# Four token groups per z tile, a 64-column product ahead of a run of 256, and backward order in every second tile

## The chip, the cores and the metric

The kernel runs on one core of a Trainium2 chip. A core has TensorE (matrix products into PSUM), VectorE, ScalarE and GpSimd, each with its own instruction stream, and SyncE, which like ScalarE issues DMA transfers. The metric is the device time of one execution in microseconds (us). The kernel before took 1241.5 us in the median of three runs, 1241.24 to 1242.45. Outputs are compared with a JAX reference.

## The reference, cut to what matters

One layer with two parallel token mixers, then a feed-forward part. 1024 tokens and 16 meta tokens make T = 1040 rows of width 1024.

```python
h = layer_norm(concat(meta, x))
z = h @ w_in + b_in                       # 1040 x 1024 by 1024 x 3840
q, k, v, c_in, gates = split(z)           # 512 | 128 | 128 | 1024 | 2048 columns
y_attn = swa_sink_attention(q, k, v, ...) @ w_attn_proj
c = c_val * sigmoid(c_gate)               # c_val, c_gate = split(c_in)
y_conv = silu(layer_norm(causal_dwconv(c, 31 taps))) @ w_conv_proj
mixed = sigmoid(g_attn) * y_attn + sigmoid(g_conv) * y_conv
h = layer_norm(alpha * h + mixed @ w_out)
f = (gelu(gate) * up) @ ffn_w_down        # up, gate from causal_dwconv(h @ ffn_w_up, 3 taps)
out = layer_norm(alpha * h + f)[16:]
```

The change lies in `z = h @ w_in` and in the two projections to `y_attn` and `y_conv`.

## The kernel before, in words

**Products.** Every fp32 operand is split into a high part and a low part in the type fp32r, and a product is three matmuls: high by high, high by low, low by high. `product` (L294) does this for a list of terms into one PSUM tile, and a matmul brings its own weight load of 128 x 128. In the trace the three are L298, L302 and L303.

**z.** The 3840 columns of z are 30 tiles of 128. A tile holds its weights still and moves the tokens, so its result has 128 partitions and a column for each token. The normalised input lies transposed in SBUF in 8 chunks of 128 features, high and low parts, chunks 0 to 3 in `RHO` and 4 to 7 in `RHC`; `h0` (L255) gives the slice of a chunk for a range of tokens. The tokens are cut into three groups, `HG` = 0 to 272, 272 to 656, 656 to 1040 (L54). Three tiles (k, v, the first q) are computed at the start in a hand-written order. The other 27 go through `z_tile` (L313), which takes the groups in order, and `z_group` (L306), which runs 8 chunks by 3 matmuls into one of three PSUM buffers (tag "mm") and then calls an eviction. The 27 are eight tiles of the convolution's input (`conv_chunk`, L640: a gate through tanh on ScalarE, then a product with it on VectorE into `cin`), three tiles of q (`q_evac`, L347) and sixteen gate tiles (`gate_tile`, L665: tanh on ScalarE into a staging slot, then a store to `sgd` from ScalarE's DMA queue). Gate and q tiles use `TG` (L321), where the first group starts at token 14 and has 258 columns. `stage` (L325) hands out five staging slots of 400 columns in turn.

**Order.** Instructions stand in each engine's stream as a scheduler puts them, by the priority in `tc.cur_priority` or `rank` and its own times. Attention runs over 8 blocks of 128 queries and two head groups, and its matmuls (`ps_s` scores, `ps_t` transposes, `ps_o` values) are interleaved with those of z tiles, which have the lower rank. `ahead` (L744) names a matmul of the first gate tile behind which the first score matmuls are put. Behind the attention come the rest of the gate tiles, and with them the layer norm of the convolution (`ps_m`).

**Projections.** For each of eight columns m of 128 output features, `branch` (L1122) runs 4 terms (12 matmuls) for the attention branch and 12 for the convolution branch, for each of the four groups of `PG` (258, 256, 256, 256 columns); `merge` (L1130) applies the gates. The tile is `ps_p`. The last column runs all its attention groups first.

**Behind it**, untouched: the product with w_out (`ps_w`), the up-projection by a fast scheme of seven products per tile (`px`, `pz`, `pw`, `py`, L1552, runs of 258 and 256 columns), and the down-projection (L1696, 512 columns).

Of the kernel before, what the change touches and what calls it, by code (L numbers as in the profile page):

```python
# [31 lines left out]
KC = D // P  # L32
# [3 lines left out]
U0 = 14  # L36
# [17 lines left out]
HG = [(0, 272), (272, 656), (656, 1040)]  # L54
UG = [(0, 258), (258, 642), (642, 1026)]

PG = [(0, 258), (258, 514), (514, 770), (770, 1026)]


HW = 514  # L60
# [40 lines left out]
def tile_hybrid_layer(  # L101
# [3 lines left out]
    nc = tc.nc  # L105
# [36 lines left out]
    FA = arena.tile([P, 6144], F, name="FA")  # L142
    RHC = arena.tile([P, 8320], R, name="RHC")
    RHO = arena.tile([P, 8320], R, name="RHO")
# [22 lines left out]
    start = ExitStack()  # L167
# [85 lines left out]


    def h0(k, hl, a, b):  # L255
        g = next(g for g, x in enumerate(HG) if a < x[1])
        x, y = HG[g]
        i, n = (k % 4) * 2 + hl, y - x
        o = i * n + ((6144 if i else 0), 272, 3344)[g]
        return (RHO if k < 4 else RHC)[:, o + a - x:o + b - x]  # L260


    tc.cur_priority = RK_QKV
# [27 lines left out]

    chunks_done = []

    def product(ps, terms, behind=None):  # L294

        n = len(terms)
        for i, (ah, al, bh, bl) in enumerate(terms):
            ins = nc.tensor.matmul(ps, ah, bh, start=i == 0, stop=False)  # L298
            chunks_done.append(ins)
            if i == 0 and behind is not None:  # L300
                after(ins, behind)
            nc.tensor.matmul(ps, ah, bl, start=False, stop=False)  # L302
            last = nc.tensor.matmul(ps, al, bh, start=False, stop=i == n - 1)  # L303
        return last

    def z_group(wt, g, a, b, evac):  # L306
        hi, lo = wt
        ps = pat.tile([P, 512], F, name="ps_z", tag="mm", bufs=3)
        product(ps[:, :b - a], [(hi[:, k], lo[:, k], h0(k, 0, a, b), h0(k, 1, a, b)) for k in range(KC)])
        with rank(RK_EVAC):  # L310
            evac(g, a, b, ps[:, :b - a])

    def z_tile(fill, groups, evac, wt=None):  # L313
        wt = wt or weights([P, KC, P], fill)
        for g, (a, b) in enumerate(groups):
            z_group(wt, g, a, b, evac)

    def in_cols(m):
        return lambda raw: load(raw, w_z[m])

    TG = [(a + U0 if i == 0 else a, b) for i, (a, b) in enumerate(HG)]  # L321

    st_next = [0]

    def stage(n, lo=4104, cnt=5):  # L325
        i = st_next[0] % cnt
        st_next[0] += 1
        return FA[:, lo + i * 400:lo + i * 400 + n]

    tc.cur_priority = RK_QKV + 1000  # L330

# [272 lines left out]
    for a, b in ((0, 400), (400, J_LEN)):  # L604
        ps = pat.tile([P, 512], F, name="ps_v", tag="o" if a == 0 else "t", bufs=1 if a == 0 else 2)
# [5 lines left out]
    wt_c1 = [weights([P, KC, P], in_cols(m)) for m in (11, 7)]  # L611
# [28 lines left out]
    def conv_chunk(c):  # L640
        sig = {}

        def g_evac(g, a, b, ps):
            sig[g] = stage(b - a)

            nc.scalar.activation(sig[g], ps, AF.Tanh, bias=bcol(10 + c), scale=0.5)
            nc.scalar.activation(sig[g], sig[g], AF.Identity, bias=half_, scale=0.5)

        z_tile(in_cols(10 + c), HG, g_evac, wt_c1[0] if c == 1 else None)
        cin = cp.tile([P, 16 + T], F, name="cin", tag="cin")  # L650
        nc.vector.memset(cin[:, 0:16], 0.0)

        def v_evac2(g, a, b, ps):
            nc.vector.scalar_tensor_tensor(cin[:, 16 + a:16 + b], ps, bcol(6 + c), sig[g], OP.add, OP.mult)

        z_tile(in_cols(6 + c), HG, v_evac2, wt_c1[1] if c == 1 else None)
        with rank(RK_CONV + c * 100):
            for j in range(TAPS):
                wc = cdw[:, j * CH + c:j * CH + c + 1]
                if j == 0:  # L660
                    nc.vector.tensor_scalar(acc[c], cin[:, j:j + U], wc, cdwb(c), OP.mult, OP.add)
                else:
                    nc.vector.scalar_tensor_tensor(acc[c], cin[:, j:j + U], wc, acc[c], OP.mult, OP.add)  # L663
# [38 lines left out]
    ps = pat.tile([P, 512], F, name="ps_vm", tag="t", bufs=2)  # L702
# [4 lines left out]
    for q4 in range(2):  # L707
        ps = pat.tile([P, 512], F, name="ps_v4", tag="t", bufs=2)
        for i in range(4):
            c = NMETA + (q4 * 4 + i) * P  # L710
# [30 lines left out]
    tc.cur_priority = RK_Z - 500  # L741
    first_chunk = len(chunks_done)
    gate_tile(0)
    ahead = chunks_done[first_chunk + 2 * KC + 5]  # L744

    tc.cur_priority = RK_ATT

# [255 lines left out]
    def oo(r, hl, a, b):  # L1003
        return OA[:, place(r * 2 + hl, a, b)]
# [114 lines left out]
    for m in range(KC):  # L1119
        hi, lo = weights([P, KC, P], lambda raw: load(raw, w_ab[m]))  # L1120

        def branch(i, g, tag, bufs):  # L1122
            a, b = PG[g]
            ps = pat.tile([P, 512], F, name="ps_p", tag=tag, bufs=bufs)
            rhs = (oo, conv)[i]
            product(ps[:, :b - a], [(hi[:, 4 * i + k], lo[:, 4 * i + k], rhs(k, 0, a, b), rhs(k, 1, a, b))
                                    for k in range(4)])
            return ps[:, :b - a]

        def merge(g, psa, psb):  # L1130
            a, b = PG[g]
            n = b - a
            with rank(RK_EVAC):
                t = gslot()[:, :, :n]
                ins = load(t, dram(sgd, m * P * U + a, [[U, P], [KC * P * U, 2], [1, n]]))

                ta, tb = t[:, 0], t[:, 1]
                nc.vector.scalar_tensor_tensor(ta, ta, 1.0, psa, OP.add, OP.mult)
                nc.vector.scalar_tensor_tensor(tb, tb, 1.0, psb, OP.add, OP.mult)
                nc.vector.tensor_tensor(ta, ta, tb, OP.add)  # L1140
                if g == 0:
                    nc.scalar.mul(pair[:, m, 0:2], ta[:, 0:2], 0.5)
                v = ta[:, n - 256:].rearrange("p (t x) -> p t x", t=2)
                h = mixed2(g, m, 0)
                last_act = nc.scalar.mul(h, v, 0.5)
                nc.vector.scalar_tensor_tensor(mixed2(g, m, 1), v, 0.5, f32(h), OP.mult, OP.subtract)
            return ins, last_act

        if m < KC - 1:
            for g in range(4):  # L1150
                last_gate, last_act = merge(g, branch(0, g, "mm", 3), branch(1, g, "t", 2))
        else:
            pa = [branch(0, g, "mm", 3) if g < 3 else branch(0, g, "s", 2) for g in range(4)]
            for g in range(4):
                last_gate, last_act = merge(g, pa[g], branch(1, g, "t", 2))
        if m in (2, 3):
            raw = (FA[:, 4112:5136], OB[:, 3072:4096])[m - 2]
            load(raw, w_out_v[m + 2])
            prep_wo(m + 2, raw, last_act)
        if m < 4:  # L1160
            early.append(FA[:, W_AT[m]:W_AT[m] + 1024])
            wo_raw[m] = early[m]
            after(load(early[m], w_out_v[m]), last_gate)
        if m > 1:
            with rank(RK_PROJ + 3000):
                two_rows(m - 2)
# [261 lines left out]
    ahead = []  # L1428
# [422 lines left out]
```

## Time and profile before

| | |
|---|---|
| median of 3 runs | 1241.5 us |
| the profiled execution | 1241.26 us |
| its span (first to last instruction) | 1239.5 us |
| TensorE busy | 1229.4 us, 8540 matmuls |
| VectorE busy | 1084.0 us |
| ScalarE busy | 580.0 us |
| z tiles through `z_tile` | about 56 to 408 us of the span |
| of these, interleaved with attention | about 162 to 327 us |
| projections | about 408 to 503 us |

A row of the timeline gives start (us), duration (us), engine, line, operation, output<-inputs, weights, moved operand (partitions x columns), and how many equal instructions in a row it merges. A matmul's duration reaches over the start of the next ones, since they are pipelined; the spacing of starts is what it costs in a stream. "PEld" rows are the weight loads. In the view of waits, a row is engine, tile and line, what it waited for, the total in us, how often, and the longest. In the view by groups, "x48 | 26.1, 543 | 47.7" reads: 48 instructions, 26.1 us busy, 543 ns in the mean, 47.7 us of idle time before them. The mark "(x...)" in the list of engines counts instructions.

### The profile page before, as it was taken

The page shows a single profiled execution, that of the slowest core. Times are in us where ns is not written, and L with a number is a line of the kernel's source. Part 1 is how long each engine was busy: PE and PEld are TensorE (multiplying, and loading weights), DVE is VectorE, ACT ScalarE, POOL GpSimd, SP SyncE. Part 2 cuts the span into 40 slices and gives each one's busy share as a digit, 9 for nine tenths or more (in the row PEclk, how much of TensorE's full clock was granted, in tenths as well). Part 3 has the DMA queues.
Part 4 walks back from the last instruction along what each step waited for, and adds up shares of the span by engine and source line. Part 5 has one row for each costly group of instructions (what it writes and reads, how often), then busy time and mean ns, then how long its engine had stood idle before and what let it go on. Part 6 is the DMA issues. An engine that isn't in the chain of part 4 may idle for free.

```text
span 1239.5 us, 21702 instructions
## 1 busy us (share of the span) xinstructions
PE 1229.4 (99%) x8540; PEld 1170.7 (94%) x8540; DVE 1084.0 (87%) x1846; ACT 580.0 (47%) x1047; POOL 12.7 (1%) x11
## 2 busy tenths in 40 slices
PE   9999999999999999999999999999999999999997
PEld 8999999999999999888999999999999998888885
DVE  7899989999978798659899999998999986995697
ACT  7532336654255323344755555455454454544330
POOL 0000000000000010000000000000000000000000
PEclk9999999999999999999999999999999999999999
DMA  7287844412255554222145555544455469987722
GB/s 283 67 300 152 199 115 107 132 37 90 75 164 154 168 165 140 102 87 85 52 171 203 205 179 213 182 176 153 162 203 194 176 239 319 391 320 290 255 85 85
DMA packets 109024, 213.08 MB, mean 172 GB/s; under 512 B 31739, under 2 KB 48683, under 8 KB 108794
## 3 DMA queue, kind: packets, MB, share of 16 engines
q1 hardware_dynamic: 93002, 200.63, 49.1%
q10 hardware_dynamic: 15920, 11.07, 2.9%
q8 instruction: 67, 1.10, 0.4%
q14 instruction: 35, 0.29, 0.1%
HBM read 150.04 MB, written 62.70 MB: 172 GB/s over the span
## 4 chain that ended last, share of the span: by engine, by line
PE 98%; DVE 1%; ACT 0%; issue 0%; DVEq 0%
PE px L1552 14%; PE py L1552 9%; PE ps_x L1696 9%; PE ps_z L302 8%; PE ps_z L298 8%; PE ps_z L303 8%; PE ps_z L1696 7%; PE pw L1552 5%; PE pz L1552 5%; PE ps_p L298 2%; PE ps_p L303 2%; PE ps_p L302 2%; PE ps_w L303 2%; PE ps_w L298 2%; PE ps_w L302 2%; PE ps_z L512 2%
## 5 line engine op out<-in xcount | busy, mean ns | idle before, releaser
L663 DVE SCALAR_TENSOR_TENSOR FA<-cin,cols,FA 128x1026 f32<-128x1026 f32 x120 | 152.1, 1278 | 0.9
L303 PE MATMUL ps_z<-RHO,wlo 128*128 128x384 f32 (+2 forms) x324 | 104.1, 321 | 0.0
L298 PE MATMUL ps_z<-RHO,whi 128*128 128x384 f32 (+2 forms) x324 | 103.9, 321 | 0.0
L302 PE MATMUL ps_z<-RHO,whi 128*128 128x384 f32 (+2 forms) x324 | 103.9, 321 | 0.0
L303 PE MATMUL ps_z<-RHC,wlo 128*128 128x384 f32 (+2 forms) x324 | 103.8, 320 | 0.0
L302 PE MATMUL ps_z<-RHC,whi 128*128 128x384 f32 (+2 forms) x324 | 103.7, 320 | 0.0
L298 PE MATMUL ps_z<-RHC,whi 128*128 128x384 f32 (+2 forms) x324 | 103.6, 320 | 0.0
L269 ACT CAST whi<-wr 128x1024 fp32r<-128x1024 f32 x37 | 38.9, 1051 | 88.7 <-PE ps_z L302 69.2
L1361 ACT CAST RHO<-wr 128x512 fp32r<-128x512 f32 x92 | 55.3, 619 | 26.2 <-DMA wr<-in_w_up_dram 12.3
L1362 DVE TENSOR_TENSOR RHO<-wr,RHO 128x512 fp32r<-128x512 f32 x92 | 61.9, 684 | 5.3 <-ACT RHO L1361 5.3
L298 PEld LDWEIGHTS ps_z<-RHO,whi 128*128 128x128 f32 x324 | 61.0, 188 | 0.1
L298 PEld LDWEIGHTS ps_z<-RHC,whi 128*128 128x128 f32 x324 | 61.1, 189 | 0.0
L303 PEld LDWEIGHTS ps_z<-RHO,wlo 128*128 128x128 f32 x324 | 61.0, 188 | 0.0
L302 PEld LDWEIGHTS ps_z<-RHO,whi 128*128 128x128 f32 x324 | 61.0, 188 | 0.0
L302 PEld LDWEIGHTS ps_z<-RHC,whi 128*128 128x128 f32 x324 | 61.0, 188 | 0.0
L303 PEld LDWEIGHTS ps_z<-RHC,wlo 128*128 128x128 f32 x324 | 60.9, 188 | 0.0
L1379 DVE TENSOR_TENSOR wr<-wr 128x512 f32<-128x512 f32 x88 | 60.1, 683 | 0.2
L272 DVE TENSOR_TENSOR wlo<-wr,whi 128x1024 fp32r<-128x1024 f32 x35 | 42.6, 1218 | 11.2 <-ACT whi L269 11.1
L670 ACT ACTIVATE FA<-ps_z,cols 128x384 f32<-128x384 f32 (+1 forms) x48 | 26.1, 543 | 47.7 <-PE ps_z L303 39.8
L1564 ACT COPY FA<-px 128x514 f32<-128x514 f32 (+2 forms) x23 | 13.1, 571 | 72.3 <-PE px L1552 72.2
L1361 ACT CAST ws<-wr 128x512 fp32r<-128x512 f32 x60 | 36.1, 618 | 17.0 <-DVE wr L1379 10.7
L1552 PE MATMUL px<-OA,RHO 128*128 128x258 f32 (+1 forms) x336 | 43.9, 279 | 0.0
(466 smaller groups left out, 3478.0 us busy)
## 6 DMA issues: line engine op xcount, KB each, us to landing
wr<-in_w_up_dram SPq DMA_DIRECT2D x44, 512.0 KB, 4.5
wr<-in_w_z_dram SPq DMA_DIRECT2D x30, 512.0 KB, 4.1
fd<-FA SPq DMA_DIRECT2D x44, 256.0 KB, 2.4
OB<-in_w_down_dram SPq DMA_DIRECT2D x19, 512.0 KB
qt<-qd SPq DMA_DIRECT2D x28, 256.0 KB, 4.2
sgd<-FA ACTq DMA_DIRECT2D x32, 192.0 KB, 3.0
td<-OB SPq DMA_DIRECT2D x12, 512.0 KB
sums<-fd SPq DMA_DIRECT2D x12, 512.0 KB, 7.0
```

The lines of the kernel that those rows point to most:

```text
L269: ins = nc.scalar.copy(hi, raw)
L272: return (nc.vector if quick else nc.gpsimd).tensor_tensor(lo, raw, f32(hi), OP.subtract)
L298: ins = nc.tensor.matmul(ps, ah, bh, start=i == 0, stop=False)
L302: nc.tensor.matmul(ps, ah, bl, start=False, stop=False)
L303: last = nc.tensor.matmul(ps, al, bh, start=False, stop=i == n - 1)
L663: nc.vector.scalar_tensor_tensor(acc[c], cin[:, j:j + U], wc, acc[c], OP.mult, OP.add)
L670: nc.scalar.activation(t, ps, AF.Tanh, bias=bcol(14 + i), scale=0.5)
L1361: nc.scalar.copy(hi, src)
L1362: ins = nc.vector.tensor_tensor(lo, src, f32(hi), OP.subtract)
L1379: ins = nc.vector.tensor_tensor(*x)
L1552: ins = nc.tensor.matmul(o, x[:, ks], bmat(sub, q, hl, k), start=first and k + j == 0, stop=k == 3 and j == 2, skip_group_check=not first)
L1696: nc.tensor.matmul(banks[i], l[:, ts], r[:, ws], start=first and a and x + k == 0, stop=z and x == len(ops) - 1 and k == 2, skip_group_che ...
```

## The change

z goes by four groups, `ZG` = 0 to 272, then three of 256 columns (gate and q tiles: 14 to 272, then the same), in place of three. `h0` places each chunk's columns from 272 on as one stretch of 768. `tiles_done` counts the tiles, and every second one takes its groups backward, from the last to the first. `product` has a new argument `lead`: a slice of 64 columns that is multiplied by the first term's weights into the first 64 columns of the PSUM tile, ahead of the product's own first matmul, which starts the sum afresh and so overwrites it. It is given for group 1 of the tiles that go forward. Staging has seven slots of 286 columns for the small groups, and `ahead` is moved by one group of 8 terms. In the projections, columns 1, 3 and 5 take their groups backward, and the attention branch of group 1 has a lead in the other columns.

```diff
+ZG = [(0, 272), (272, 528), (528, 784), (784, 1040)]
...
     def h0(k, hl, a, b):
-        g = next(g for g, x in enumerate(HG) if a < x[1])
-        x, y = HG[g]
-        i, n = (k % 4) * 2 + hl, y - x
-        o = i * n + ((6144 if i else 0), 272, 3344)[g]
-        return (RHO if k < 4 else RHC)[:, o + a - x:o + b - x]
+        i = (k % 4) * 2 + hl
+        if a < 272:
+            o = i * 272 + (6144 if i > 2 else 0)
+        else:
+            o = 816 + i * 768 - 272
+        return (RHO if k < 4 else RHC)[:, o + a:o + b]
...
-    def product(ps, terms, behind=None):
+    def product(ps, terms, behind=None, lead=None):
...
+        if lead is not None:
+            nc.tensor.matmul(ps[:, :64], terms[0][0], lead, start=True, stop=True)
...
-    def z_group(wt, g, a, b, evac):
+    def z_group(wt, g, a, b, evac, lead):
...
-        product(ps[:, :b - a], [(hi[:, k], lo[:, k], h0(k, 0, a, b), h0(k, 1, a, b)) for k in range(KC)])
+        product(ps[:, :b - a], [(hi[:, k], lo[:, k], h0(k, 0, a, b), h0(k, 1, a, b)) for k in range(KC)],
+                lead=h0(0, 0, 0, 64) if lead else None)
...
+    tiles_done = [0]
+
     def z_tile(fill, groups, evac, wt=None):
         wt = wt or weights([P, KC, P], fill)
-        for g, (a, b) in enumerate(groups):
-            z_group(wt, g, a, b, evac)
+        back = tiles_done[0] % 2
+        tiles_done[0] += 1
+        for g, (a, b) in list(enumerate(groups))[::-1 if back else 1]:
+            z_group(wt, g, a, b, evac, g == 1 and not back)
...
-    TG = [(a + U0 if i == 0 else a, b) for i, (a, b) in enumerate(HG)]
+    TG = [(a + U0 if i == 0 else a, b) for i, (a, b) in enumerate(ZG)]
...
-    def stage(n, lo=4104, cnt=5):
-        i = st_next[0] % cnt
-        st_next[0] += 1
-        return FA[:, lo + i * 400:lo + i * 400 + n]
+    def stage(n):
+        big = n > 272
+        cnt, size = ((7, 286), (5, 400))[big]
+        o = 4136 + st_next[big] % cnt * size
+        st_next[big] += 1
+        return FA[:, o:o + n]
...
-    ahead = chunks_done[first_chunk + 2 * KC + 5]
+    ahead = chunks_done[first_chunk + 2 * KC + 5 + KC]
...
-                                    for k in range(4)])
+                                    for k in range(4)],
+                    lead=oo(0, 0, 0, 64) if i == 0 and g == 1 and not back else None)
...
+        back = m in (1, 3, 5)
         if m < KC - 1:
-            for g in range(4):
+            for g in range(3, -1, -1) if back else range(4):
```

`conv_chunk` passes `ZG` in place of `HG` to both of its tiles. The three tiles at the start keep `HG`.

More of the change, by code (lines that the diff above doesn't have):

```diff
@@ L304, in product @@
         return last
-    def z_group(wt, g, a, b, evac):
+    def z_group(wt, g, a, b, evac, lead):
         hi, lo = wt
         ps = pat.tile([P, 512], F, name="ps_z", tag="mm", bufs=3)
-        product(ps[:, :b - a], [(hi[:, k], lo[:, k], h0(k, 0, a, b), h0(k, 1, a, b)) for k in range(KC)])
+        product(ps[:, :b - a], [(hi[:, k], lo[:, k], h0(k, 0, a, b), h0(k, 1, a, b)) for k in range(KC)],
+                lead=h0(0, 0, 0, 64) if lead else None)
         with rank(RK_EVAC):
             evac(g, a, b, ps[:, :b - a])
+    tiles_done = [0]
     def z_tile(fill, groups, evac, wt=None):
         wt = wt or weights([P, KC, P], fill)
-        for g, (a, b) in enumerate(groups):
-            z_group(wt, g, a, b, evac)
+        back = tiles_done[0] % 2
+        tiles_done[0] += 1
+        for g, (a, b) in list(enumerate(groups))[::-1 if back else 1]:
+            z_group(wt, g, a, b, evac, g == 1 and not back)
     def in_cols(m):
         return lambda raw: load(raw, w_z[m])
-    TG = [(a + U0 if i == 0 else a, b) for i, (a, b) in enumerate(HG)]
-    st_next = [0]
-    def stage(n, lo=4104, cnt=5):
-        i = st_next[0] % cnt
-        st_next[0] += 1
-        return FA[:, lo + i * 400:lo + i * 400 + n]
+    TG = [(a + U0 if i == 0 else a, b) for i, (a, b) in enumerate(ZG)]
+    st_next = [0, 0]
+    def stage(n):
[4 more added lines that the diff above has]
+        return FA[:, o:o + n]
     tc.cur_priority = RK_QKV + 1000
@@ L647, in g_evac @@
             nc.scalar.activation(sig[g], sig[g], AF.Identity, bias=half_, scale=0.5)
-        z_tile(in_cols(10 + c), HG, g_evac, wt_c1[0] if c == 1 else None)
+        z_tile(in_cols(10 + c), ZG, g_evac, wt_c1[0] if c == 1 else None)
         cin = cp.tile([P, 16 + T], F, name="cin", tag="cin")
@@ L654, in v_evac2 @@
             nc.vector.scalar_tensor_tensor(cin[:, 16 + a:16 + b], ps, bcol(6 + c), sig[g], OP.add, OP.mult)
-        z_tile(in_cols(6 + c), HG, v_evac2, wt_c1[1] if c == 1 else None)
+        z_tile(in_cols(6 + c), ZG, v_evac2, wt_c1[1] if c == 1 else None)
         with rank(RK_CONV + c * 100):
```

## The prediction

> **What bounds the kernel now.** I read the page first: the engines, the granted clock by slices, the chain of work that ended last.
>
> ```profile
> PE 1229.4 (99%) x8540; PEld 1170.7 (94%) x8540; DVE 1084.0 (87%) x1846; ACT 580.0 (47%) x1047; POOL 12.7 (1%) x11
> PEclk9999999999999999999999999999999999999999
> PE 98%; DVE 1%; ACT 0%; issue 0%; DVEq 0%
> ```
>
> 98% of the closing chain is TensorE, at full clock throughout. Then the waits of TensorE, the whole list:
>
> ```profile
> PE ps_w L536 <- DVE sel L1087: 1.1, 1, 1.1
> PE pw L1552 <- DVE OA L1237: 0.4, 1, 0.4
> PE ps_z L509 <- ACT FA L468: 0.3, 1, 0.3
> ```
>
> None lies in the z tiles or the projections, the two stages that change. So time there is the sum of the spacings between matmul starts, and nothing else; what a spacing gains or loses goes straight into the end. Busy time is no help, because records of overlapping matmuls overlap; I read starts. One whole gate tile, the timeline of TensorE (24 matmuls of 258 columns, 48 of 384, then the next tile):
>
> ```profile
> 102.79 0.28 PE L298 MATMUL ps_z<-RHO,whi 128*128 128x258 f32 x1
> ...
> 105.69 0.34 PE L298 MATMUL ps_z<-RHO,whi 128*128 128x384 f32 x1
> ...
> 114.01 0.28 PE L298 MATMUL ps_z<-RHO,whi 128*128 128x258 f32 x1
> ```
>
> 258 columns: 2.90 us / 24 = 120.8 ns. 384 columns: 8.32 / 48 = 173.3 ns. Now 256 columns, in the projections: two stretches of equal work (72 and 60 matmuls, first row to the row after the last):
>
> ```profile
> 410.91 0.28 PE L298 MATMUL ps_p<-OA,whi 128*128 128x256 f32 x1
> ...
> 419.39 0.28 PE L298 MATMUL ps_p<-OA,whi 128*128 128x258 f32 x1
> ...
> 422.29 0.29 PE L298 MATMUL ps_p<-OA,whi 128*128 128x256 f32 x1
> ...
> 429.10 0.28 PE L298 MATMUL ps_p<-OA,whi 128*128 128x258 f32 x1
> ...
> 495.53 0.39 PE L298 MATMUL ps_w<-RX,RHC 128*128 128x512 f32 x1
> ```
>
> 8.48 / 72 = 117.8 ns, but 6.81 / 60 = 113.5 ns. The same shape has **two speeds**, and a run keeps the one it has. The up-projection shows it again, with rows that hold 12 matmuls each:
>
> ```profile
> 592.98 0.39 PE L298 MATMUL ps_w<-RW,RHO 128*128 128x512 f32 x1
> ...
> 593.66 1.58 PE L1552 MATMUL px<-OC,W 128*128 128x256 f32 x12
> ...
> 597.90 0.60 PE L1331 MATMUL py<-cols,OB 128*128 128x128 f32 x4
> 598.34 0.60 PE L1331 MATMUL pz<-cols,OB 128*128 128x128 f32 x4
> 598.69 1.64 PE L1552 MATMUL pw<-RHC,RHO 128*128 128x256 f32 x12
> 599.48 0.84 PE L1552 MATMUL pw<-RHC,RHO 128*128 128x256 f32 x6
> 600.16 1.61 PE L1552 MATMUL py<-OC,RHO 128*128 128x256 f32 x12
> ```
>
> Behind the 512-column matmuls: 4.24 us / 36 = 117.8 ns (593.66 to 597.90). Behind the short 128-column transposes: the last six of twelve take 0.68 / 6 = 113.3 ns (599.48 to 600.16). So the entry decides: from long matmuls slow; from 258 columns both ways (slow from 410.91, fast from 422.29); from short ones, the single row there is, fast after some six matmuls.
>
> **The change part by part.** (1) A z tile has 24 matmuls of 272 or 258 columns as before, and 72 of 256 in place of 48 of 384. At 113.3 that is 8.16 us against 8.32, a gain of 0.16 a tile; at 117.8 it is 8.48, a loss of 0.16. There are 27 tiles, 1944 matmuls of 256 columns. In the built program's order 1373 of them stand in runs of 40 or more (mostly 144, two tiles back to back, which is what the backward order makes), and 571 in some 58 pieces among the attention's matmuls. Long runs, fast: 1373 x 113.3 = 155.6 us, in place of 915 x 173.3 = 158.6: -3.0. Slow: 161.7, +3.1.
>
> The pieces have about ten matmuls each, and enter from short attention matmuls or from 256 columns; with the settling of 598.69 (six in 0.79 us, 131.7 ns) and 113.3 after it, ten take 1.24 us. That counts an excess at the entry, 0.11 us, of which a piece of 384 pays a part too:
>
> ```profile
> 223.18 0.35 PE L303 MATMUL ps_z<-RHC,wlo 128*128 128x384 f32 x1
> 223.38 0.27 PE L807 MATMUL ps_r<-cols,rall 128*24 128x128 f32 x1
> ```
>
> Here a 384 behind short matmuls holds the engine 0.20 us instead of 0.173. I take 115.5 a matmul, between the two speeds, for what differs: 571 x 115.5 = 66.0 against 381 x 173.3 = 66.0: 0. Bounds 113.3 and 117.8: -1.3 to +1.3.
>
> (2) **The 64-column products.** The built program has 19: 14 in z (every forward tile) and 5 in the projections. No such matmul is in the trace. Its nearest row is the 8-column one:
>
> ```profile
> 187.24 0.28 PE L798 MATMUL ps_o<-p,va 80*128 80x8 f32 x2
> 187.38 0.37 PE L298 MATMUL ps_z<-RHO,whi 128*128 128x272 f32 x1
> ...
> 187.71 0.38 PE L870 MATMUL ps_t<-cols,s 128*128 128x128 f32 x2
> ```
>
> From 187.24 to 187.71 are two 8-column matmuls and two of 272; with 272 columns at about 0.125 (an estimate, the 120.8 of 258 columns plus 14 columns at the 0.42 ns a column between the 384 and 512 rows), the short ones cost (0.47 - 0.25) / 2 = 0.11 us each: something other than columns, the weight load that each brings, sets the floor. Settled as in the row at 598.69: entry (0.35 us from 598.34, less three transposes at 0.44 / 4 = 0.11) 0.02, plus 0.79 - 6 x 0.1133 = 0.11, together 0.13. I take 0.11, nearest in shape: 19 x 0.11 = +2.1. Bounds 0.03 (64 of 256 columns of 113.3, if the weight load were hidden) and 0.13: +0.6 to +2.5.
>
> The Trainium skill ("TensorE: Matmul & The Clock Gate", section "Back-to-back issue gap") gives N / 2.4 + 2.5 ns for a matmul's spacing. By it a 64-column product would be 29 ns, the 19 together an estimated 0.6 us; the 8-column row, at 0.11, disagrees. By the same rule two 384s would be 325 ns and three 256s 327.5, so that the split loses an estimated 1.6 us over 27 tiles before any lead. Rows of 173.3 and 113.3 disagree, in the direction that favours the change.
>
> (3) Projections. From the first one to 495.53 lie 744 matmuls, 192 of 258 and 552 of 256 columns:
>
> ```profile
> 408.02 0.28 PE L298 MATMUL ps_p<-OA,whi 128*128 128x258 f32 x1
> ```
>
> 87.51 - 192 x 0.1208 = 64.3 us, or 116.5 ns for one of 256: a mix of both speeds, seven tenths slow. In the new order 540 of them follow a lead or adjoin such a run: fast, 540 x (113.3 - 116.5) = -1.7; slow, +0.7.
>
> (4) The rest rides on other engines. Evictions:
>
> ```profile
> L670 ACT ACTIVATE FA<-ps_z,cols 128x384 f32<-128x384 f32 x31 | 17.9, 578 | 32.8 <-PE ps_z L303 24.9 <-DMA sgd<-FA 7.4 <-ACT FA L670 0.5
> L670 ACT ACTIVATE FA<-ps_z,cols 128x258 f32<-128x258 f32 x16 | 7.6, 473 | 14.9 <-PE ps_z L303 14.8
> ```
>
> A gate tile now has four of about 0.47 (1.88 us) for 0.47 + 2 x 0.58 (1.63): +0.25 on ScalarE, 16 times, and one store more on its queue. ScalarE is busy for 47% of the span. VectorE gets one piece more in the four cin tiles and three query tiles, about 0.17 each by the same step, 1.2 us in all; TensorE, which has z tiles left after the last attention matmul in the new order too, hides it. Without that cover it is at most +1.2. The 7 staging slots of 286 replace 5 of 400; a wait for a store (7.4 us in two cases) stands ahead of the tile's next eviction on ScalarE, and is paid only if the PSUM ring runs dry (rival three). The moved operands keep their sizes, and the initial tiles their 384s. Cost 0.
>
> Sum: -3.0 + 0 + 2.1 - 1.7 = -2.6. The profiled execution took 1241.26 us (span 1239.5), so 1238.7; the median of the runs, 1241.5, stands 0.24 above it, so on that scale **1238.9 us, and I say 1238.8** because the lead's lower bound leaves more room below its value than its upper bound above.
>
> **The rivals.** One: the lead locks the runs to the slow speed. For it: the slow speed is what long matmuls and stalls leave behind, and a lead drains nothing. Against it: the one short entry went fast. Then z +3.1 + 1.3, projections +0.7, leads +2.1: +7.2, 1248.7, decided at the first 256-column start behind the first lead. Two: the lead decides nothing and each run draws its own speed, as from 258 columns now. At 115.5: long runs 158.6 against 158.6, 0; projections 540 x (115.5 - 116.5) = -0.5; leads +2.1; sum +1.6, with the luck of 19 draws about +-1.5: 1243.1. Three: the ring of three PSUM buffers. The latest eviction now:
>
> ```profile
> 377.13 0.28 PE L303 MATMUL ps_z<-RHC,wlo 128*128 128x258 f32 x1
> 381.15 0.46 ACT L670 ACTIVATE FA<-ps_z,cols 128x258 f32<-128x258 f32 x1
> ```
>
> It ends 4.5 us after its group's last start. Two groups of 24 x 0.1133 leave 5.4 us where two of 24 x 0.1733 left 8.3. It fits by 0.9; one more eviction and store ahead of it (0.8) would just touch. Price under 1 us, 1239.5. Four: spacing is linear in columns, and 256 inside z behaves like its neighbours: 512 columns take 0.68 / 3 = 226.7 ns (592.98 to 593.66), which with 173.3 gives 13.3 ns a matmul plus 0.417 a column, or 120.0 for 256: z 1944 x 120.0 = 233.3 against 224.6, +8.7, leads +2.1: 1252.3. Both measured speeds speak against it. The Trainium skill's rule, named above, has this form with a smaller constant.
>
> **How the numbers follow.** Forecast 0.63, rival one 0.24, two 0.08, three 0.03, four 0.02. The forecast's own range, from the bounds (fragments +-1.3, leads -1.5 to +0.4), is 1236.0 to 1240.5. A measurement of this kernel tells about 0.2% (2.5 us) from no change, so faster means under 1239.0: of the forecast's 0.63 I give 0.43 to that and 0.20 to "same". Rival two gives 0.05 to same and 0.03 to slower (over 1244.0), three 0.03 to same, one and four are slower. Faster 0.43, same 0.28, slower 0.29. The range takes in the forecast's own, rivals two and three, and half of rival one: 1236.0 to 1248.5.
>
> **What would show it.** In the timeline of the new kernel, first 256-column start to next 272 or 258 start, over 144: 16.3 us if fast, 17.0 if slow. Two gate tiles: 22.2 us if fast (48 x 0.1208 + 16.32 + 0.11), against 22.44. The start behind a 64-column product's, and the one after, together about 0.22 us. Still no TensorE wait on ScalarE or VectorE in z. I am wrong if the first run behind a lead reads 117 to 118 ns, or if TensorE waits show L302 to L307 with more than 1 us.

## The result and the profile after

The changed kernel takes **1246.24 us** in the median of seven runs (1243.93 to 1246.67); the kernel before, run beside it, 1241.76 (seven runs, 1241.24 to 1243.12). The ratio is 1.0029, with a 95% interval of 1.0017 to 1.0040: slower by 0.2 to 0.4%, where 1238.8 had been forecast. The profiled execution took 1246.56 us, its span is 1244.8. From the page of the changed kernel, the engines, the granted clock in 40 slices, the chain that ended last:

```profile
PE 1229.5 (99%) x9207; PEld 1171.0 (94%) x9207; DVE 1086.5 (87%) x1853; ACT 588.2 (47%) x1078; POOL 13.2 (1%) x11
PEclk9999999999999999999999999999999999999999
PE 93%; DVE 3%; DMA 3%; ACT 0%; issue 0%; SPq 0%; DVEq 0%
```

TensorE's busy time is unchanged to 0.1 us, but its share of the closing chain fell from 98% to 93%, and DMA stands in it with 3%. The clock line looks full; each of its digits covers 31 us, so a short drop doesn't show. The longest waits of TensorE in the changed kernel:

```profile
PE ps_s L845 <- DMA qt<-qd: 2.1, 1, 2.1
PE ps_h L473 <- DVE xn L437: 1.6, 1, 1.6
PE ps_z L302 <- DVE cin L665: 1.4, 1, 1.4
```

None of the three stands in the list of before. The first and the third lie in z. The second lies in the start, ahead of all that changed; in the other profiles of this study it is 0.2 to 1.4 us or not in the list, also where the start is the same (1.3 us and none in the two kernels that change the projections alone). The stages by their first rows, the timeline of the changed kernel (first z matmul of `z_tile`, first of the projections, first of the up-projection), and the one row of before that the prediction doesn't show:

```profile
57.10 0.37 PE L302 MATMUL ps_z<-RHO,whi 128*128 128x272 f32 x1
...
414.60 0.28 PE L302 MATMUL ps_p<-OA,whi 128*128 128x258 f32 x1
...
599.08 0.40 PE L1565 MATMUL px<-OC,W 128*128 128x256 f32 x2
```

```profile
56.51 0.37 PE L298 MATMUL ps_z<-RHO,whi 128*128 128x272 f32 x1
```

| stage | before, us | changed, us | difference |
|---|---|---|---|
| up to the first z tile | 56.51 | 57.10 | +0.59 |
| z tiles with attention | 351.51 | 357.50 | **+5.99** |
| projections and product with w_out | 185.64 | 184.48 | **-1.16** |

The three add to +5.4, and the spans differ by 5.3. So the projections gave what was forecast, and z lost 6 us.

**Where z lost it: three places.** First, TensorE of the changed kernel around 78 us; a row's bracket gives the idle time ahead of it and what ended that:

```profile
77.22 0.28 PE L307 MATMUL ps_z<-RHC,wlo 128*128 128x256 f32 x1
78.86 0.39 PE L302 MATMUL ps_z<-RHO,whi 128*128 128x272 f32 x1 [1.37 <-DVE cin L665]
```

VectorE of the changed kernel in the same stretch:

```profile
77.20 1.21 DVE L456 TENSOR_TENSOR OB<-OB,gb 128x1024 f32<-128x1024 f32 x1
78.34 1.25 DVE L665 SCALAR_TENSOR_TENSOR cin<-ps_z,cols,FA 128x256 f32<-128x256 f32 x3
```

And VectorE of the kernel before, at the same point of the work:

```profile
75.47 2.34 DVE L445 TENSOR_TENSOR OB<-OB,gb 128x1024 f32<-128x1024 f32 x2
77.75 1.01 DVE L654 SCALAR_TENSOR_TENSOR cin<-ps_z,cols,FA 128x272 f32<-128x272 f32 x2
```

The tile is the second half of convolution column 1. Its groups are evicted by VectorE, which in both kernels is busy with the normalisation (`OB`) until about 78 us and then evicts several groups at once: three of 256 columns now, two before (the row of before merges one of 272 columns and one of 384). A tile of three groups fits the ring of three PSUM buffers while nobody empties it; a tile of four does not, and its fourth group, the 272 columns, waits: 1.64 us from start to start, 1.5 more than a usual spacing.

Second, block 0 of the attention. Timeline of TensorE, changed kernel:

```profile
144.23 0.28 PE L307 MATMUL ps_z<-RHC,wlo 128*128 128x256 f32 x1
146.65 1.09 PE L845 MATMUL ps_s<-kx,qt 128*128 128x80 f32 x8 [2.15 <-DMA qt<-qd]
```

2.42 us from start to start, 2.3 lost. (The row merges eight score matmuls, four of 80 and four of 144 columns.) In the kernel before, the first score matmul starts at 140.74 us and waits for nothing. The chain of waits of the changed kernel (start, duration, what) names two transfers ahead of it:

```profile
135.39 4.42 DMA qd<-qsl
141.11 5.41 DMA qt<-qd
```

VectorE of the changed kernel makes the piece that is stored last before them:

```profile
134.57 0.42 DVE L364 TENSOR_TENSOR qsl<-FA,qsh 128x258 fp32r<-128x258 f32 x1
```

SyncE's queue of the changed kernel, the first load of queries:

```profile
139.93 0.50 SPq L113 DMA_DIRECT2D qt<-qd  x1
```

The same two in the kernel before, VectorE:

```profile
131.06 0.42 DVE L353 TENSOR_TENSOR qsl<-FA,qsh 128x258 fp32r<-128x258 f32 x1
```

and SyncE's queue:

```profile
134.60 1.78 SPq L112 DMA_DIRECT2D qt<-qd  x3
```

A query's low part goes from VectorE by a store (`qd`) to DRAM and comes back by a load (`qt`). The last q tile's first group (258 columns), which the first scores need, was made at 131.06 and is now made at 134.57. Of these 3.5 us TensorE itself brings 2.5: it starts that group at 127.73 instead of 125.23. The q tile ahead of it runs backward, so that tile's first group comes last, and VectorE makes its low part at 131.84, next ahead of the other one. The store that was issued at 135.39 lands 4.42 us later, and the first load is issued at 139.93 instead of 134.60, 5.3 us later than before. The scores would have started some 0.1 us behind 144.23, only 3.6 us later than before, so they come before the queries. There was little to spare: the kernel with the projections' part alone, below, has the z order of before, and its first scores already wait 0.2 us for `qt`. No run turned the order of the q tiles alone, so how much of this the backward order costs is not shown.

Third, the clock. Busy time and granted clock by stretches of the changed kernel (stretch, length, PE, PEld, DVE, ACT, POOL, then the clock):

```profile
144.51:146.65 2.14, 0.00 (x0) 0.03 (x1) 2.14 (x3) 0.47 (x1) 0.00 (x0) 1.00 0.98 266
146.65:148.10 1.45, 1.45 (x13) 1.45 (x13) 1.27 (x6) 0.00 (x0) 0.00 (x0) 1.00 1.12 294
148.10:151.50 3.40, 3.40 (x19) 3.40 (x18) 3.40 (x6) 0.00 (x0) 0.00 (x0) 0.50 1.04 220
151.50:155.00 3.50, 3.50 (x43) 3.46 (x43) 1.76 (x4) 0.48 (x1) 0.00 (x0) 1.00 0.77 167
```

TensorE's starts in the third of these stretches:

```profile
148.29 0.42 PE L307 MATMUL ps_z<-RHO,wlo 128*128 128x256 f32 x1
...
151.50 0.29 PE L307 MATMUL ps_z<-RHC,wlo 128*128 128x256 f32 x1
```

After the idle stretch the clock stays full for 1.45 us, then is granted at one half for 3.4 us: 15 matmuls in 3.21 us, 214 ns each instead of 113, with the one ahead of them 1.6 us lost. 1.5 + 2.3 + 1.6 = 5.4 of z's 6.0.

The 1.45 us can be read from the trace's clock records. In the changed kernel they run from 4.74 to 148.10 us at full clock, to 151.52 at half and to 1240.37 at full: 42, 1 and 319 stretches of 3.413 us; in the kernel before from 6.79 to 1235.59 at full, 360 such stretches. So in these traces the clock changes only at the ends of such stretches, and the drop begins at the end of the one from 144.69 to 148.10, in which TensorE was idle for 1.96 us. The idlest stretch with no drop behind it, from 8.16 us in the same trace, has 1.60 us.

**What the leads did.** Timeline of the changed kernel, two gate tiles toward the end of the attention:

```profile
314.93 0.19 PE L300 MATMUL ps_z<-RHO,whi 128*128 128x64 f32 x1
314.96 0.36 PE L302 MATMUL ps_z<-RHO,whi 128*128 128x256 f32 x1
315.16 0.28 PE L306 MATMUL ps_z<-RHO,whi 128*128 128x256 f32 x1
...
331.38 0.28 PE L302 MATMUL ps_z<-RHO,whi 128*128 128x258 f32 x1
...
337.13 0.19 PE L300 MATMUL ps_z<-RHO,whi 128*128 128x64 f32 x1
```

The same timeline, two earlier runs of 144:

```profile
85.47 0.37 PE L302 MATMUL ps_z<-RHO,whi 128*128 128x256 f32 x1
...
102.52 0.28 PE L302 MATMUL ps_z<-RHO,whi 128*128 128x272 f32 x1
...
108.45 0.36 PE L302 MATMUL ps_z<-RHO,whi 128*128 128x256 f32 x1
...
124.86 0.28 PE L302 MATMUL ps_z<-RHO,whi 128*128 128x258 f32 x1
```

144 matmuls take 16.42 us from 314.96 and 16.41 from 108.45: the fast speed. From one lead to the next, two tiles, are 22.20 us. But the 144 from 85.47, whose lead stands behind 272 columns, take 17.05: slow, although a lead is there.

### The profile page after: what moved, and what is told of

It is laid out like the page before. It is cut to its first block, busy times and chain, and to the rows that moved or that the text cites. A ratio compares the mean times of both kernels' runs of the same rounds, so it can differ in the third digit from the quotient of the medians.

```text
span 1244.8 us, 23108 instructions
## 1 busy us (share of the span) xinstructions
PE 1229.5 (99%) x9207; PEld 1171.0 (94%) x9207; DVE 1086.5 (87%) x1853; ACT 588.2 (47%) x1078; POOL 13.2 (1%) x11
## 4 chain that ended last, share of the span: by engine, by line
PE 93%; DVE 3%; DMA 3%; ACT 0%; issue 0%; SPq 0%; DVEq 0%
PE px L1565 14%; PE py L1565 9%; PE ps_x L1709 9%; PE ps_z L1709 7%; PE ps_z L302 7%; PE ps_z L306 7%; PE ps_z L307 7%; PE pw L1565 5%; PE pz L1565 5%; PE ps_p L302 2%; PE ps_p L306 2%; PE ps_p L307 2%; PE ps_w L302 2%; PE ps_w L307 2%; PE ps_w L306 2%; PE ps_z L523 2%
## 5 line engine op out<-in xcount | busy, mean ns | idle before, releaser
L302 PE MATMUL ps_z<-RHO,whi 128*128 128x256 f32 (+2 forms) x432 | 122.8, 284 | 1.4 <-DVE cin L665 1.4
L306 PE MATMUL ps_z<-RHC,whi 128*128 128x256 f32 (+2 forms) x432 | 122.1, 283 | 0.0
L306 PE MATMUL ps_z<-RHO,whi 128*128 128x256 f32 (+2 forms) x432 | 121.6, 282 | 0.0
L307 PE MATMUL ps_z<-RHC,wlo 128*128 128x256 f32 (+2 forms) x432 | 121.6, 282 | 0.0
L302 PE MATMUL ps_z<-RHC,whi 128*128 128x256 f32 (+2 forms) x432 | 121.6, 281 | 0.0
L307 PE MATMUL ps_z<-RHO,wlo 128*128 128x256 f32 (+2 forms) x432 | 121.5, 281 | 0.0
L302 PEld LDWEIGHTS ps_z<-RHO,whi 128*128 128x128 f32 x432 | 81.5, 189 | 1.6 <-DVE cin L665 1.6
L307 PEld LDWEIGHTS ps_z<-RHC,wlo 128*128 128x128 f32 x432 | 81.8, 189 | 0.0
L307 PEld LDWEIGHTS ps_z<-RHO,wlo 128*128 128x128 f32 x432 | 81.8, 189 | 0.0
L306 PEld LDWEIGHTS ps_z<-RHC,whi 128*128 128x128 f32 x432 | 81.8, 189 | 0.0
L302 PEld LDWEIGHTS ps_z<-RHC,whi 128*128 128x128 f32 x432 | 81.7, 189 | 0.0
L306 PEld LDWEIGHTS ps_z<-RHO,whi 128*128 128x128 f32 x432 | 81.7, 189 | 0.0
L681 ACT ACTIVATE FA<-ps_z,cols 128x256 f32<-128x256 f32 (+1 forms) x64 | 30.2, 471 | 71.9 <-PE ps_z L307 53.2
```

Source lines behind the costliest of these rows:

```text
L681: nc.scalar.activation(t, ps, AF.Tanh, bias=bcol(14 + i), scale=0.5)
```

## The experiments

Of the kernels named here, "the change" is the one above. Times are medians of eleven runs (eight for one kernel, a single run for the change again), and each ratio is to the kernel before on the same chip.

**Theory after the result:** the 256-column matmuls took their faster speed, and the loss is the two waits and the drop of the clock behind the second. **Rivals:** the waits only show a loss that 256 columns in z cost anyway; the leads do nothing.

### Scores later

Only an order among TensorE's instructions is added to the change, no wait.

```diff
+    later = chunks_done[first_chunk + 3 * KC + 1]
...
+                        if i == 0:
+                            after(ins, later)
```

`ins` is a score matmul of block 0.

> The changed kernel with one more order: the score matmuls of block 0 stand behind the 26th of the 32 terms of gate tile 0, about 2.7 us of products later than now, past the point (146.65 us) where the transposed queries had landed. Theory (two waits of TensorE, and the halved clock that follows the second, make the loss): the 2.4 us wait of ps_s for qt goes, the clock stays at 1.00 from 146 to 162 us, and with that 2.3 + 1.65 us: 1246.2 becomes about 1242.3, and the spread of the runs shrinks to that of the kernel before. Rival (short pieces, slow runs and leads inside the attention make the loss, and a wait removed is replaced by the next one): 1245.5 to 1246.5, with a new wait of about 2 us later in the attention.

Measured: 1242.68 us (1242.39 to 1244.66), ratio 1.0010 (1.0001 to 1.0019), 3.6 less than the change. Two of TensorE's waits are left in z:

```profile
PE ps_z L302 <- DVE cin L665: 1.4, 1, 1.4
...
PE ps_z L302 <- ACT FA L681: 0.9, 1, 0.9
```

The clock in the stretches that had the stall and the drop:

```profile
144.00:148.00 4.00, 4.00 (x38) 4.00 (x37) 4.00 (x5) 0.95 (x2) 0.00 (x0) 1.00 1.06 274
148.00:152.00 4.00, 4.00 (x47) 3.96 (x47) 4.00 (x9) 0.88 (x1) 0.00 (x0) 1.00 1.02 246
```

The wait for `qt` is gone and the clock stays full in the profiled execution. 2.3 + 1.6 = 3.9 was at stake; 0.9 of it comes back as a wait at 373 us, where z tiles run between the layer norm's matmuls and ScalarE empties the ring (L681), near the place that rival three of the prediction had looked at. That leaves 3.0 where the medians show 3.6; the 0.6 is not assigned.

### Three groups in convolution column 1

```diff
-        z_tile(in_cols(10 + c), ZG, g_evac, wt_c1[0] if c == 1 else None)
+        z_tile(in_cols(10 + c), HG if c == 1 else ZG, g_evac, wt_c1[0] if c == 1 else None)
...
-        z_tile(in_cols(6 + c), ZG, v_evac2, wt_c1[1] if c == 1 else None)
+        z_tile(in_cols(6 + c), HG if c == 1 else ZG, v_evac2, wt_c1[1] if c == 1 else None)
```

The two tiles have no lead.

> The changed kernel, but the two z tiles of convolution column 1 go by the three groups of before (272, 384, 384), with no lead. Theory: these tiles fill the ring of three PSUM buffers once per tile, so the 1.4 us wait of ps_z for cin at 78 us goes: about -1.5 us, +0.3 for two tiles without runs of 256; 1246.2 becomes about 1245.0. The wait for the queries stays, if no cover of it moves. Rival (the wait only moves to the next tile): 1246.2 to 1246.5, with a wait of 1 to 2 us on cin before 90 us.

Measured: 1243.48 us (1242.38 to 1247.40), ratio 1.0021 (1.0011 to 1.0030). In the profiled execution, 1242.55 us, the wait for `cin` is gone, as expected, and the one for `qt`, which had been expected to stay, is halved:

```profile
PE ps_s L845 <- DMA qt<-qd: 1.0, 1, 1.0
...
PE ps_z L302 <- ACT FA L681: 0.9, 1, 0.9
```

The runs lie 5 us apart, and the longest, 1247.40, shows a mean granted clock of 0.995 where the profiled one shows 0.999: this fits a drop behind the queries' wait that comes in some executions and not in others.

### Both

The two edits above together.

> Both edits. Theory: neither wait, full clock, what is left is the spacing of the matmuls: 1240.5 to 1241.2, as fast as the kernel before or faster by up to 1 us. Rival: 1245 or more.

Measured: 1241.11 us (1240.85 to 1242.76), ratio 0.9996 (0.9987 to 1.0005). 5.1 us less than the change, and the runs are close together again. z with its attention takes 352.05 us, against 351.51 before. Of the waits in z only the one on L681 is left, 0.9 us. So the waits and the drop made the loss, the first rival falls; and with all but one of them gone z is still no faster than before.

### The projections' part alone, with and without leads

The kernel before, with the backward columns 1, 3 and 5 and the leads of the projections; then the same with `lead=None`.

> The kernel before, with the projections' part of the change alone (backward order in columns 1, 3, 5, and five 64-column products). Theory: the runs of 256 go at 113.3 ns, 540 x 3.2 = 1.7 us less, five leads of 0.11 more: 1241.7 becomes 1240.5. Rival (the lead eats the gain, and the 1.2 us less in that stage of the changed kernel came from elsewhere): 1241.5 to 1242.

> The kernel before with the backward order in projection columns 1, 3 and 5 and no 64-column products. Theory: the five long runs draw their speed from the phase of the 258 columns ahead of them, at least one goes at 117.8 ns: 1240.7 plus 0.6 us for each slow run of 144, less 0.55 for the leads: 1240.1 if none is slow, 1241.9 if three are. Rival (backward order alone makes the gain): 1240.1 with all runs at 113.3.

Measured: with leads 1240.69 us (1240.18 to 1241.43), ratio 0.9992 (0.9984 to 1.0001); without 1242.27 (1241.74 to 1242.89), ratio 1.0003 (0.9994 to 1.0012). Timeline of the kernel with leads:

```profile
411.41 0.36 PE L300 MATMUL ps_p<-OA,whi 128*128 128x256 f32 x1
...
427.82 0.28 PE L300 MATMUL ps_p<-OA,whi 128*128 128x258 f32 x1
...
592.97 0.40 PE L1556 MATMUL px<-OC,W 128*128 128x256 f32 x2
```

Timeline of the kernel without:

```profile
411.35 0.28 PE L300 MATMUL ps_p<-OA,whi 128*128 128x256 f32 x1
...
428.31 0.28 PE L300 MATMUL ps_p<-OA,whi 128*128 128x258 f32 x1
...
594.75 0.40 PE L1556 MATMUL px<-OC,W 128*128 128x256 f32 x2
```

144 matmuls in 16.41 us, with a lead, against 16.96, or 117.8 ns each, without. All five runs are fast with leads and all five slow without. Up to the first of these runs the order of TensorE is the same in both kernels; behind it the second kernel moves 12 matmuls in two columns. So behind 258 columns the lead decides, and in the projections the second rival falls. The price of a lead is seen too: five leads at 0.13 make 0.65 us, the 540 faster matmuls save 540 x 4.5 ns = 2.4, and the difference of 1.8 is that of the two up-projection starts.

### Both edits, no leads at all

The kernel of "both" with every `lead` taken out.

> The kernel with both edits (scores later, big groups in column 1), without any of its 64-column products, in z and in the projections. Theory (a lead behind 258 columns sets the fast speed, and costs 0.11 us): without it a run of 256 behind 258 draws its speed, so some of the ten long runs (about 130 matmuls each) go at 117.8 ns, 0.6 us more for each that does, while 18 leads save 2.0 us; if about half are slow, +3.0 - 2.0, 1242.1 against 1241.1. Rival (the runs go fast on their own when both neighbours are 256 runs, the lead is only a cost): 1239.1, and every long run at 113.3.

Measured: 1241.82 us (1241.25 to 1243.01), ratio 1.0001 (0.9992 to 1.0010). Long runs of 256 are now a mix: those from about 128, 330 and 400 us are slow, and so are the 56 from 364 us, behind 384 columns; the others are fast, and in the projections three are slow and two fast. Without leads a run draws its speed, as rival two of the prediction supposed for runs with them. By the two ratios the 18 leads of "both" are worth 0.6 us, within the intervals. By the stages of the two profiles that is the projections' (184.49 us with leads, 185.09 without); z takes 352.05 with them and 352.15 without, so in z no gain of the leads is shown.

### The change again, and the scores between

The change once more, and the order of "scores later" with the scores 5 products earlier (`2 * KC + 4` for `3 * KC + 1`), to see a shorter stall.

> The changed kernel once more, unaltered, one look. Its seven runs lay at 1243.9 to 1244.6 with a mean granted clock of 0.998, and at 1245.6 to 1246.7 with 0.997 or 0.998. Theory: the wait for the queries is in every execution, the halved clock behind it only in some, so this profile shows either 1246 to 1247 with a stretch of 0.5 behind 147 us, or 1244 to 1244.8 without it. Rival (the spread comes from waits of different length, not from the clock): the time and the wait move together, with no relation to the clock.

> The changed kernel with the scores of block 0 behind the 21st of the 32 terms of gate tile 0, about 1.3 us of products later than in the changed kernel, 1.4 earlier than in the kernel with the scores later. Theory: a wait of about 1.0 us for the queries stays, too short to lower the clock as a rule: 1242.7 + 1.0 = 1243.7 in most runs, and 1.7 more in those where the clock drops. Rival (any wait costs the clock): 1245.4 in all runs.

Measured: the change 1246.27 us. Its stall is 2.4 us, of which 1.97 fall into the last stretch of 3.413 us ahead of the drop, and the drop is there as before:

```profile
148.00:152.00 4.00, 4.00 (x23) 4.00 (x23) 4.00 (x8) 0.00 (x0) 0.00 (x0) 0.58 1.04 226
```

Scores between: 1244.58 us (1243.07 to 1246.58), ratio 1.0022 (1.0013 to 1.0031). The profiled execution, 1243.20, has a wait for `qt` of 0.3 us, where about 1.0 had been expected, and a full clock; the three longest runs, 1245.97 to 1246.58, show a mean clock of 0.997, the others 0.998 or 0.999. So the drop may come or not at this place. From the traces, it came behind stretches with 1.96 and 1.97 us idle and not behind 1.60; whether a stall lies in one stretch or is shared by two may be what decides from run to run, but no run shows that.

This kernel shows one thing more. In z its order on TensorE is that of the change up to here, and its 144 matmuls behind 272 columns and a lead, which took 17.05 us in the change, are fast. The timeline of the scores between:

```profile
85.58 0.36 PE L302 MATMUL ps_z<-RHO,whi 128*128 128x256 f32 x1
...
102.00 0.29 PE L302 MATMUL ps_z<-RHO,whi 128*128 128x272 f32 x1
```

16.42 us. So behind 272 columns even a run with a lead draws its speed.

### The operands' places alone

The kernel before with the changed kernel's `h0` and nothing else: same instructions, same order on TensorE, other SBUF columns for the z operands.

> The kernel before with the new places of the z operand's columns (one stretch of 768 for both groups of 384) and nothing else; the order of TensorE's instructions is the same. Theory from the kernel with four groups behind the attention alone: behind 258 columns the 384s go at 176.8 ns in the new places, in place of 173.3: 19 tiles x 48 x 3.5 ns = 3.2 us less what is cut up by the attention, so 1241.7 becomes 1244 to 1245. Rival (places do not matter; those spacings came from the order of work): 1241.7.

Measured: 1244.78 us (eight runs, 1244.18 to 1245.58), ratio 1.0027 (1.0016 to 1.0037). One gate tile's 384s, the timeline of this kernel:

```profile
106.11 0.34 PE L299 MATMUL ps_z<-RHO,whi 128*128 128x384 f32 x1
...
114.59 0.28 PE L299 MATMUL ps_z<-RHO,whi 128*128 128x258 f32 x1
```

8.48 us / 48 = 176.7 ns, where the same 48 took 8.32, or 173.3, before. Over all 1296 the mean spacing is 177.3 against 175.2 ns, +2.7 us, and TensorE has no wait in the z tiles. So where an operand lies costs the 384-column matmuls 2.7 us, and a kernel that keeps three groups under the new `h0`, even in some tiles, pays a part of it.

### Four groups only behind the attention, and a mixture

First only nine of the gate tiles by four groups, all others by three, `ahead` as before. Here the two sets of staging slots overlap in SBUF, so that a value of the convolution's gate is overwritten and the output is not the reference's; only its time is read. Then the mixture: convolution tiles and the two gate tiles among the layer norm's matmuls (11 and 12) by three groups, q tiles and the other fourteen gate tiles by four, "scores later", one set of five staging slots, projections as changed.

```diff
-        z_tile(in_cols(10 + c), ZG, g_evac, wt_c1[0] if c == 1 else None)
+        z_tile(in_cols(10 + c), HG, g_evac, wt_c1[0] if c == 1 else None)
...
-        z_tile(in_cols(6 + c), ZG, v_evac2, wt_c1[1] if c == 1 else None)
+        z_tile(in_cols(6 + c), HG, v_evac2, wt_c1[1] if c == 1 else None)
...
-        z_tile(in_cols(14 + i), TG, gate_evac)
+        z_tile(in_cols(14 + i), TG3 if i in (11, 12) else TG, gate_evac)
```

`TG3` is `TG` made from `HG`. The diff is that of the mixture against the change, without the staging slots and the order of the scores. In both kernels the tiles of three groups run forward, have no lead and are not counted for the order of the others.

> The four groups and their leads only in nine gate tiles, 5 to 10 and 13 to 15, most of them behind the attention; the other z tiles, with the query and convolution tiles, by the three groups of before in forward order; the projections as in the changed kernel. Theory: no wait on the queries, on cin or on the ring at 373 us, full clock; nine tiles gain 0.16 each and pay five leads of 0.11, about -0.7 with pieces among the attention's last matmuls; projections -1.0: about 1240.0, faster than the kernel before by 1.2 to 2.0 us. Rival (four groups gain nothing once waits are out, all gain is the projections'): 1240.7, as the kernel with the projections' part alone.

> Four groups and leads in the query tiles and fourteen gate tiles, with the scores of block 0 later; the eight convolution tiles (272 columns in the first group) and gate tiles 11 and 12 by the three groups of before; one ring of five staging slots; the projections as in the changed kernel. Theory (a lead behind 258 columns always sets the fast speed, waits were the loss): no wait over 0.5 us of a z or score matmul, every lead fast, and against the kernel with the projections' part alone (1240.7) a gain of 17 tiles x 0.1 less pieces and two slow tiles of 384: 1239.5 to 1240.3. Rival (cutting z into more pieces gives back what the spacing gains): 1240.7 or more.

Measured: only behind the attention 1240.84 us (1240.62 to 1241.16), ratio 0.9993 (0.9984 to 1.0002); no wait in z, but z takes 352.28 us, and the time is the rival's. The 864 matmuls of 384 columns that are left run at 177.7 ns in the mean; against the 175.2 of before that is about 2.2 us for the operands' places, an estimate from the two means. The mixture: **1239.47 us** (1239.04 to 1240.09), ratio 0.9981 (0.9972 to 0.9990), faster than both kernels. The whole list of TensorE's waits of 0.3 us or more in it:

```profile
PE ps_w L545 <- DVE sel L1099: 1.1, 1, 1.1
PE pw L1566 <- DVE OA L1251: 0.4, 1, 0.4
PE ps_h L471 <- DVE xn L435: 0.4, 1, 0.4
PE ps_z L518 <- ACT FA L477: 0.3, 1, 0.3
```

None of these lies in `z_tile` (L518 is one of the three tiles at the start). z takes 350.92 us, 0.6 less than before, with 1224 matmuls of 256 at 115.5 ns and 480 of 384 at 176.9; the projections stage takes the same 184.48 as in the change. At 176.9 against 175.2 those 480 still pay some 0.8 us for the operands' places, an estimate from the two means.

## Why the prediction was wrong

**What failed is step (4), "The rest rides on other engines ... Cost 0".** With four groups in every tile the other engines cost 5.4 us, in three places: VectorE's eviction at 78 us (1.5), the queries at 144 us (2.3), and the clock (1.6). The working priced VectorE's extra pieces by their own duration (0.17 us each) and named as cover the z tiles behind the last attention matmul. But a piece on VectorE is not paid where TensorE ends; it is paid where TensorE next needs it. Two consumers were not followed: the PSUM ring while VectorE is in a long normalisation, and the chain VectorE, store, load, score of the queries, which had next to no time to spare. "Scores later", "three groups in column 1" and "both" take these away one by one and give 3.6, 2.8 (with a wide spread) and 5.1 us back. The spans differ by +5.3 us where the sum had -2.6; these 5.4 and the 2.2 of step (1), below, are nearly all of the 7.9 between them. The price of the clock could not be read from the profile of before, which has no such drop while TensorE works. The Trainium skill ("TensorE: Matmul & The Clock Gate", "Part 1: The HAM clock gate") puts the half clock behind at least one idle window of about 3.4 us. The length of the drop here, 3.4 us, agrees with that window; the idle time does not, since a stall of 2.14 us, of which 1.96 lay in the stretch before the drop, was enough.

**The range held by luck.** 1246.24 lies inside 1236.0 to 1248.5 because the range took in half of rival one, and rival one's cause, leads that lock the slow speed, is not what made the loss.

**Rival three had the mechanism and the wrong place.** The ring of three buffers was checked at 377 us on ScalarE, and found to fit by 0.9 us. The tight place was on VectorE at 78 us. The check at 377 us was itself near: with the earlier stalls gone, 0.9 us of wait shows at 373 us.

**Step (1), long runs fast, -3.0: right in kind, too large.** 1021 of the 1373 matmuls in runs of 40 or more ran fast. 352 did not: 196 in the two runs whose lead stands behind 272 columns, 100 that enter from 256-column attention matmuls and 56 from 384-column ones of the layer norm. 352 x 4.5 ns = 1.6 us. By the sums of spacings, without the waits and the drop, the 1944 matmuls of 256 took 227.2 us and the 14 leads 0.5 (what settles behind a lead is in the runs), against 227.0 for the 1296 of 384: +0.7, where (1) and the 14 leads gave -3.0 + 1.5 = -1.5. 1.6 of these 2.2 us are those 352 matmuls. The rest is in the short pieces: 120.8 ns in the mean without the drop, where 115.5 had been put, 571 x 5.3 ns = 3.0 us; the 384s of before paid 2.4 of the kind too, 227.0 for the 224.6 of 173.3 each.

**Step (2), the leads, +2.1: right.** A lead takes 0.03 us and its run 16.42 instead of 144 x 0.1133 = 16.32, together 0.13, the upper end of what was given; 19 make 2.5. The two gate tiles at 22.20 us met the forecast of 22.2, and the two starts behind a lead, 0.23 us together, that of 0.22.

**Step (3), projections: right.** -1.7 and five leads at 0.11 make -1.15; -1.16 was measured, and the part alone gave the median 1.0 us.

**Rivals one, two and four.** One, that the lead locks the slow speed, is refuted behind 258 columns, where every long run with a lead was fast, and by the pair with and without leads; behind 272 columns three of four such stretches of the changed kernel were not fast. Two holds where no lead stands and, by the two times of the stretch at 85 us, behind 272 columns with a lead. Four, 120 ns for 256 columns, is refuted by every long run: 113 or 118. The rule N / 2.4 + 2.5 ns that the prediction takes from the Trainium skill ("TensorE: Matmul & The Clock Gate", "Back-to-back issue gap") stands there for an isolated matmul; in the kernels here each matmul brings its weight load, so the rows that disagree with it are of another case.

**Of the signs that were named,** "Still no TensorE wait on ScalarE or VectorE in z" was wrong. Both signs of a wrong forecast came true: L302 waits 1.4 us, with the transfer's wait on the scores beside it, and the first run behind a lead, 52 matmuls from 60.23 us behind 272 columns, goes at 118 ns. The first sign is what broke the forecast; the second, with the run from 85.47, is worth 196 x 4.5 ns = 0.9 us.

## What to carry to other kernels

Splitting a tile into more groups is not free on the engines that empty it: count the groups that are in flight while the slowest evictor is away, and compare that with the buffers of the ring, at every place and for every evictor. When an order is turned round, follow what used to come first through its stores and loads to the matmul that needs it. Then place the faster form only where no such consumer is near: the mixture won 2.5 us with the same idea that lost 4.5 when it was applied to every tile. By the stages of its profile 0.6 of that lie in z and 1.2 in the projections.

## What the runs showed of the hardware

- 256-column fp32r matmuls run at 113.3 or 117.8 ns, and a long run mostly keeps what it has. One longer spacing can end the fast speed: in the kernel before, the matmul at 600.16 us takes 153 ns, and the 256-column ones behind it go on at 118. Behind 258 columns a 64-column product brought the fast speed in every run of twelve or more that followed it at once, in all profiles. Behind 272 columns it failed in three of four stretches of the change, and one of these was fast in another kernel. Without it all five projection runs were slow in one kernel and three of five in another. What sets the speed was not found.
- The place of a moved operand in SBUF alone changed the spacing of 384-column matmuls from 173.3 to 176.7 ns and the kernel by 3.2 us. Which columns do it was not tried.
- A stall of 2.14 us cost TensorE not only that: 1.45 us after it ended, at the end of a stretch of 3.413 us with 1.96 us idle, the clock was halved for 3.4 us, which cost 1.6 us more. At this place it came in both profiles of the change. In kernels with a shorter stall the mean clocks of some runs fit such a drop; none of their profiles shows one.
